# Gate rows stored block by block, and stores moved from SyncE's queue to those of GpSimd and ScalarE, in a hybrid HGRN2, mLSTM and mixture-of-experts layer

## The chip, the core and the metric

The kernel runs on one core of a Trainium2 chip. The core has five engines with a queue of instructions each: TensorE (PE in the profile; the loading of its weights is shown apart, as PEld), VectorE (DVE), ScalarE (ACT), GpSimd (POOL) and SyncE (SP, which here only issues transfers). Transfers between the memory of the chip (DRAM) and the core's own memory run on 16 DMA engines. The metric is the device time of one execution in microseconds: 1577.56 us, the median of three runs (1577.32, 1577.56 and 1581.70).

## The reference

The layer takes 1024 latent tokens `x` and 256 context tokens, each 1024 wide. It projects them with one wide matrix, and runs two kinds of recurrence over the tokens, forward and backward, four heads of HGRN2 and four of mLSTM. The context gives the states from which the latent tokens' recurrences start. Cut to what matters here, the mLSTM is:

```python
def mlstm_scan(q, k, v, log_i, log_f, state):      # chunk by chunk, running-max stabiliser m
    ...
    b = jnp.cumsum(fc, axis=-1)
    d = jnp.where(mask, b[..., :, None] - b[..., None, :] + ic[..., None, :], -jnp.inf)
    inter = b + m[..., None]
    m_row = jnp.maximum(inter, jnp.max(d, axis=-1))
    w_inter = jnp.exp(inter - m_row)
    qk = jnp.einsum('bhid,bhjd->bhij', qc, kc) * jnp.exp(d - m_row[..., None])
    num = jnp.einsum('bhij,bhjv->bhiv', qk, vc) + w_inter[..., None] * jnp.einsum('bhid,bhdv->bhiv', qc, c)
    ...
    h = num / jnp.maximum(jnp.abs(den), jnp.exp(-m_row))[..., None]
```

What follows it:

```python
hg = _head_rms_norm(hg_o_f + hg_o_b) * silu(pr['hg_g'])         # first gates
ml = _head_layer_norm(ml_h_f + ml_h_b) * sigmoid(pr['ml_o'])    # second gates
x = x + g1 * (concat([hg, ml]) @ w_out)
v_x = rms_norm(x, norm2_w) * (1.0 + sc2) + sh2
x = x + g2 * ec_moe(v_x, ...)       # 16 experts, each takes the 128 tokens that score it highest
return rms_norm(x, final_norm_w)
```

Tokens go through the kernel in eight blocks of 128 (`cc` = 0 to 7); a chunk of the reference is half a block, and the kernel uses the same sums over whole blocks.

## The kernel before, in words

The work is staged as follows, in the order of time; TensorE works in all of them.

1. Up to 180 us: the modulation vectors, the context's projections and its final states. `ml_gates` (L389) computes, for all 1024 latent tokens, 8 directions and heads at once, the row `M` = -m_row (eight rows of 1024, kept as 64 partitions of 128) and `em` = exp(M + m), and stores them to DRAM as `d_nm` and `d_em` (L457, L461), [8 rows, 1024 tokens].
2. 180 to 500 us: the HGRN2 heads. Beside them `out_gate(0, ...)` computes the first gates, 128 tokens by 256 columns at a time, into a tile `gsg` of three buffers, and stores each with L719 to `d_go`.
3. 500 to 711 us: the convolutions, the mLSTM's values, the second gates (`out_gate(1, ...)`, L719 again), and the backward states `Sb`, one a block, which `back_u` stores to `d_sb` (L852). The list `ORD` (L1076) interleaves these. Its end takes in `S0`, `O0`, `L0` and `S1`: the first pieces of stage 4.
4. 711 to 935 us: eight rounds, one a block. `scores` (L931) loads `qkx`, `E` and `MB` for a block. `E` takes the block's 128 tokens of the eight rows of `d_nm`, spread to all 128 partitions, and `MB` the same of `d_em` (L936). ScalarE and VectorE make decays of them (L942 to L947). `outputs` (L950) multiplies them with values and states on TensorE (L972, L973) and loads one backward state (L956). `normed` (L981) takes the layer norm, whose power -0.5 GpSimd computes (`rsqrt`, L156, a tile `r4` of 4 columns). `mixed` (L995) loads the HGRN2 outputs and the gates (L998, L999) and puts both halves together. `mixer` (L1012) multiplies with `w_out` (48 matmuls at L1023), adds to `x`, and stores the block to `d_acc` (L1026). `router` (L1043) scales the block with another power on GpSimd (`r2`, 1 column), and stores the experts' input to `d_v` (L1053). In round `cc`, `scores(cc + 2)`, `outputs(cc + 1)` and `mixer(cc)` run.
5. 895 to 968 us: the sorting that picks 128 tokens for each expert. It begins within the last rounds.
6. 968 to 1580 us: the experts. Rows of `d_v` are gathered, and results added into `d_acc`, by transfers that GpSimd issues (L1315, L1311). The experts' weights (L891) are read ahead from stage 4 on into every buffer that has come free. The last rows are normed and written.

Each engine, and each queue of transfers, goes through its instructions in the order in which they stand. A transfer's issue waits in its queue until what it reads is there and its buffer is free, and what stands behind it in that queue waits too. The order within each engine is set when the program is built, by a scheduler that plays the program through with its own costs; so an edit can move instructions on engines that it doesn't name. `load` (L44) is SyncE's queue, for loads and stores alike; SyncE computes nothing. In all 16 transfers fetch `E` and `MB`, of 512 KB each, as 1024 pieces of 512 bytes: `E` and `MB` have two buffers each.

Of the kernel before, what the change touches and what calls it, by code (L numbers as in the profile page):

```python
# [9 lines left out]
F32 = mybir.dt.float32  # L10
# [9 lines left out]
P = 128  # L20
# [12 lines left out]
def tile_hybrid_block(ctx, tc, x, c, cx, c_ctx, ada_w, ada_b, norm1_w, w_in, conv_w, conv_b,  # L33
                      lb_logits, gate_b, hg_norm_w, ml_norm_w, w_out, norm2_w, router_w,
                      e_gate, e_up, e_down, final_w, out, dbg=None, stop=None):
    nc = tc.nc
# [4 lines left out]
    load = nc.sync.dma_start  # L41
# [10 lines left out]
    d_gxc = dram.tile([16, 256], F32, name="d_gxc")  # L52
    d_sb = dram.tile([8, P, 516], F32, name="d_sb")
    d_gx = dram.tile([16, 1024], F32, name="d_gx")
    d_nm = dram.tile([8, 1024], F32, name="d_nm")
    d_em = dram.tile([8, 1024], F32, name="d_em")
    d_g = dram.tile([4, 1024], F32, name="d_g")
    d_v = dram.tile([1024, 1024], F32, name="d_v")
    d_acc = dram.tile([1024, 1024], F32, name="d_acc")
# [330 lines left out]
    def ml_gates(pool):  # L390
# [62 lines left out]
        V.tensor_scalar(M, cm, mcol, None, op0=OP.max)  # L453
        V.tensor_add(b, b, M)
        V.tensor_scalar(M, M, -1.0, None, op0=OP.mult)
        for d in range(2):
            load(d_nm[4 * d:4 * d + 4].rearrange("h (c i) -> (h c) i", i=P), M[64 * d:64 * d + 32])  # L457
        em = mk("gem")
        S.activation(em, M, AF.Exp, bias=mcol)
        for d in range(2):  # L460
            load(d_em[4 * d:4 * d + 4].rearrange("h (c i) -> (h c) i", i=P), em[64 * d:64 * d + 32])  # L461
        pt = bank("ms")
        T.transpose(pt[:, 0:128], g, ident)
        T.transpose(pt[:, 128:256], b, ident)
# [186 lines left out]
    with tc.tile_pool(name="hgp", bufs=1) as hp_:  # L651
        tl = lambda name, shape, bufs: hp_.tile([P] + shape, F32, name=name, tag=name, bufs=bufs)
        fw = {}
        for h in range(4):
            if h % 2 == 0:
                wq = wload([(HG_Q + h * P, 256)])
            w = wload([(HG_FF + h * P, P), (HG_FF + 512 + h * P, P)])
            ada_next(2 if h > 1 else 1)
            F = [tl("hgf", [2, 512], 2) for _ in range(2)]
            QK = [tl("hgqk", [2, 512], 2) for _ in range(2)]  # L660
            for d in range(2):
                pf = [bank("mm"), bank("mm")]
                feat(w, d * P, (d + 1) * P, pf, uh, ul)
                for hf in range(2):
                    hg_f(hp_, F[hf], pf[hf], d, h, slice(0, 512))
            pq = [bank("mm"), bank("mm")]
            feat(wq, (h % 2) * P, (h % 2 + 1) * P, pq, uh, ul)
            for hf in range(2):
                S.activation(QK[hf][:, 1, :], pq[hf], AF.Sigmoid)
                V.tensor_mul(QK[hf][:, 0, :], QK[hf][:, 1, :], pq[hf])  # L670
            Qs, As, Us, decs = [], [], [], []
            for hf in range(2):
                f, qk = F[hf], QK[hf]
                K, Q = tl("hgK", [2, 512], 2), tl("hgQ", [2, 512], 3)
                A, U = tl("hgA", [4, P], 3), tl("hgU", [4, 2, P], 3)
                V.tensor_scalar(K, f, -1.0, 1.0, op0=OP.mult, op1=OP.add)
                V.tensor_add(qk[:, 1, :], K[:, 0, :], K[:, 1, :])
                V.tensor_mul(Q, qk[:, 0, :].unsqueeze(1).to_broadcast([P, 2, 512]), view(f, 512, [[-512, 2], [1, 512]]))
                dec = hg_tree(hp_, f, K, Q, qk, A)
                hg_u(hp_, K, lambda cc: hv[:, 4 * hf + cc, h * P:(h + 1) * P], U, ((0, 4 - hf), (1 - hf, 4)))  # L680
                Qs.append(Q), As.append(A), Us.append(U), decs.append(dec)

            def st(d, cc):

                return S0[:, d, h, :] if cc < 0 or cc > 7 else Us[cc // 4][:, cc % 4, d, :]

            for cc in range(7):
                step(st(0, cc), st(0, cc - 1), decs[cc // 4](0, cc % 4), st(0, cc))
            for cc in reversed(range(1, 8)):
                step(st(1, cc), st(1, cc + 1), decs[cc // 4](1, cc % 4), st(1, cc))  # L690
            for hf in range(2):
                po = bank("ms", [P, 4, P])
                for c4 in range(4):
                    cc = 4 * hf + c4
                    ts = slice(c4 * P, (c4 + 1) * P)
                    T.matmul(po[:, c4, :], As[hf][:, c4, :], hv[:, cc, h * P:(h + 1) * P], start=True, stop=False)
                    T.matmul(po[:, c4, :], Qs[hf][:, 1, ts], st(0, cc - 1), start=False, stop=False)
                    T.matmul(po[:, c4, :], Qs[hf][:, 0, ts], st(1, cc + 1), start=False, stop=True)
                ob = tl("hgo", [4, P], 1)
                for c4 in range(4):  # L700
                    S.activation(ob[:, c4, :], po[:, c4, :], AF.Square, scale=KSCALE,
                                 accum_out=hgr[:, 4 * hf + c4, h:h + 1])
                S.copy(ob, po)
                load(d_hg[4 * hf:4 * hf + 4, :, h * P:(h + 1) * P].rearrange("c p v -> p c v"), ob)

        def out_gate(gi, hf, w, ts):

            for t in ts:
                if gi == 0 and t % 4 == 3:
                    ada_next()  # L710
                pb = bank("mm")
                tok(w, 0, 256, pb[:, :256], t, uh, ul)
                sg = wring.tile([P, 256], F32, name="gsg", tag="gsg", bufs=3)
                if gi:
                    S.activation(sg, pb[:, :256], AF.Tanh, scale=0.5)
                else:
                    S.activation(sg, pb[:, :256], AF.Sigmoid)  # L717
                    V.tensor_mul(sg, sg, pb[:, :256])
                load(d_go[t][:, 512 * gi + 256 * hf:512 * gi + 256 * hf + 256], sg)  # L719

        for hf in range(2):
            out_gate(0, hf, wload([(HG_G + 256 * hf, 256)]), range(8))
# [121 lines left out]
    def back_u(cc):  # L844

        prev = Sbs[-1]
        Sb = tp("Sb", [4, 129], 2)
        for hp, u in enumerate(ml_u(kts.pop(cc), v1[cc])):
            for q in range(2):
                h = 2 * hp + q  # L850
                step(Sb[:, h, :], prev[:, h, :], wsx[:, cc, 1, h:h + 1], u[:, q, :])
        load(d_sb[cc], Sb.rearrange("p h v -> p (h v)"))  # L852
        Sbs.append(Sb)

    Sbs = [mlc[:, 1]]
# [75 lines left out]
    def scores(cc):  # L931

        qk, MB, E = tl("qkx", [8, P], 2), tl("MB", [8, P], 2), tl("E", [2, 4, P], 2)
        load(qk, d_qk[cc])
        for t, src in ((E.rearrange("p d h t -> p (d h) t"), d_nm), (MB, d_em)):
            load(t, bass.AP(tensor=src.tensor, offset=src.offset + cc * P, ap=[[0, P], [1024, 8], [1, P]]))  # L936
        pq = bank("hg", [P, 4, P])
        for h in range(4):
            T.matmul(pq[:, h, :], qk[:, 4 + h, :], qk[:, h, :], start=True, stop=True)
        for d in range(2):  # L940
            for h in range(4):
                S.activation(E[:, d, h, :], E[:, d, h, :], AF.Identity, bias=gT[:, cc, d, h:h + 1])  # L942
            V.tensor_tensor(E[:, d], E[:, d], cmask[:, d, :].unsqueeze(1).to_broadcast([P, 4, P]), op=OP.min)
        S.activation(E, E, AF.Exp)
        for d in range(2):
            V.tensor_mul(MB[:, 4 * d:4 * d + 4, :], qk[:, 0:4, :], MB[:, 4 * d:4 * d + 4, :])
            V.scalar_tensor_tensor(E[:, d], pq, KSCALE, E[:, d], op0=OP.mult, op1=OP.mult)  # L947
        kt = ml_k_tok(blk, lambda h: qk[:, 4 + h, :], wkx[:, cc, 0], False) if cc < 7 else None
        return E, MB, kt
# [63 lines left out]
    def mixer(cc, mh, ml_):  # L1013

        row = slice(cc * P, (cc + 1) * P)
        xm = tb("xm", [1024], 2)
        load(xm, x[row])
        for hf in range(2):
            cs = slice(512 * hf, 512 * hf + 512)
            pb = bank("mm")  # L1020
            for k in range(8):
                for q, (l, r) in enumerate(((mh, woh), (mh, wol), (ml_, woh))):
                    T.matmul(pb, l[:, k, :], r[k][:, cs], start=(k == 0 and q == 0), stop=(k == 7 and q == 2))  # L1023
            V.tensor_mul(pb, pb, g1b[:, cs])
            V.tensor_add(xm[:, cs], xm[:, cs], pb)
        load(d_acc[row], xm)  # L1026
        return xm

    def logits(xm):
# [14 lines left out]
    def router(cc, xm):  # L1044

        row = slice(cc * P, (cc + 1) * P)
        r2 = tb("r2", [1], 2)
        vt = tb("vt", [1024])
        S.activation(vt, xm, AF.Square, scale=1.0 / 32, accum_out=r2)
        rsqrt(r2, r2, 1)  # L1050
        V.scalar_tensor_tensor(vt, xm, r2, A2b, op0=OP.mult, op1=OP.mult)
        V.tensor_add(vt, vt, B2b)
        kept["v"] = load(d_v[row], vt)  # L1053
        if dbg and "xm" in dbg:
            nc.sync.dma_start(dbg["xm"][row], xm)
            nc.sync.dma_start(dbg["v"][row], vt)
        return r2
# [389 lines left out]
```

## Time and profile before

| | |
|---|---|
| median of the runs | 1577.56 us (1577.32 to 1581.70) |
| the profiled execution's own time | 1582.25 us |
| its span, first to last instruction | 1580.4 us |
| TensorE busy, matmuls | 1443.7 us (91%) |
| VectorE, ScalarE, GpSimd busy | 1231.1, 841.8 and 85.6 us |
| chain that ended last | PE 74%, DMA 11%, DVE 8% |
| two lines of that chain | `MB<-d_em` 5%, `E<-d_nm` 2% |

The profile is one execution. A line names the source line, the engine, the operation, the tile written and the tiles read (`out<-in`). Where an engine sat idle, the line names what ended the idle time, as "<-ACT whi L253"; "issue" is time in which nothing that the profile shows was waited for. The chain of waits is followed back from the last instruction. "PEclk" is the clock that TensorE was granted, as a share of its full one. "DMA share" is the mean busy share of the 16 DMA engines; beside GB/s it tells whether busy engines moved much. "SPq" is an instruction of SyncE that issues a transfer; its time is that of the issue, and not of the transfer. A busy TensorE is not TensorE at its peak, since neighbouring matmuls overlap in the records.

### The profile page before, as it was taken

What the parts mean: (1) busy time and instruction counts of PE and PEld (TensorE: products, weight loads), DVE (VectorE), ACT (ScalarE), POOL (GpSimd) and SP (SyncE); (2) the same over time, 40 slices, a digit from 0 to 9 for tenths busy, and PEclk for the clock granted to TensorE, in tenths of its full rate; (3) what the DMA queues carried; (4) which work ended last, traced back from release to release, by engine and by line L of the source; (5) the groups of instructions that cost most, each with busy time, mean ns of one, the idle gap of its engine ahead of it and who ended that gap; (6) DMA issues with size and microseconds to landing.
All of it is one profiled execution on the core that took longest, in us unless ns stands there. A gap on an engine that the chain in (4) does not pass through costs nothing.

```text
span 1580.4 us, 23097 instructions
## 1 busy us (share of the span) xinstructions
PE 1443.7 (91%) x8121; PEld 1202.8 (76%) x8121; DVE 1231.1 (78%) x2223; ACT 841.8 (53%) x1431; POOL 85.6 (5%) x96
## 2 busy tenths in 40 slices
PE   7999999999999999868676965999999999999996
PEld 2899888888898887856565843888888888888774
DVE  3685477888768788447545796999999999998887
ACT  3764434334423323235333323877777878777765
POOL 0000000000020000000000000000100000000003
PEclk9999999999999999979798986999999999999998
DMA  9741311121235343587774386999999999999942
GB/s 258 259 129 31 109 54 54 55 81 55 80 119 162 107 132 115 156 148 221 219 139 152 135 302 215 358 383 384 378 378 386 387 388 386 386 381 357 354 146 107
DMA packets 189616, 341.53 MB, mean 216 GB/s; under 512 B 13720, under 2 KB 116764, under 8 KB 189500
## 3 DMA queue, kind: packets, MB, share of 16 engines
q1 hardware_dynamic: 184888, 324.22, 59.8%
q0 software_dynamic: 4320, 15.73, 4.2%
q8 instruction: 64, 1.05, 0.3%
q14 instruction: 52, 0.43, 0.1%
q10 hardware_dynamic: 292, 0.10, 0.0%
HBM read 307.58 MB, written 32.42 MB: 215 GB/s over the span
## 4 chain that ended last, share of the span: by engine, by line
PE 74%; DMA 11%; DVE 8%; issue 4%; ACT 2%; POOL 1%; SPq 0%; ACTq 0%; POOLq 0%; DVEq 0%
PE mm L1300 21%; PE mm L279 14%; PE mm L287 11%; PE hg L1300 10%; DMA MB<-d_em 5%; PE hg L351 4%; DMA E<-d_nm 2%; PE hg L216 2%; PE ms L1285 2%; DMA sb<-d_sb 1%; PE ms L383 1%; PE mm L1023 1%; PE mm L500 1%; PE hg L1390 1%; PE mm L972 1%
## 5 line engine op out<-in xcount | busy, mean ns | idle before, releaser
L287 PE MATMUL mm<-whi,uh 128*128 128x256 f32 (+1 forms) x512 | 145.4, 284 | 1.5 <-DVE utmp L199 0.9
L287 PE MATMUL mm<-whi,ul 128*128 128x256 f32 (+1 forms) x512 | 145.0, 283 | 0.0
L287 PE MATMUL mm<-wlo,uh 128*128 128x256 f32 (+1 forms) x512 | 144.9, 283 | 0.0
L254 DVE TENSOR_TENSOR wlo<-wraw,whi 128x512 fp32r<-128x512 f32 x96 | 64.9, 689 | 44.9 <-ACT whi L253 43.4
L287 PEld LDWEIGHTS mm<-whi,uh 128*128 128x128 f32 x512 | 96.7, 189 | 3.5 <-DVE utmp L199 1.1
L287 PEld LDWEIGHTS mm<-whi,ul 128*128 128x128 f32 x512 | 96.8, 189 | 0.0
L287 PEld LDWEIGHTS mm<-wlo,uh 128*128 128x128 f32 x512 | 96.3, 188 | 0.3
L826 DVE SCALAR_TENSOR_TENSOR cacc<-pad,cols,cacc 128x1024 f32<-128x1024 f32 x64 | 81.8, 1281 | 14.3 <-ACT cacc L824 13.5
L1300 PE MATMUL mm<-qkx,xT 128*128 128x512 f32 x256 | 83.7, 408 | 0.6 <-ACT xT L1286 0.3
L253 ACT CAST whi<-wraw 128x512 fp32r<-128x512 f32 x96 | 58.3, 620 | 47.1 <-PE mm L279 31.3
L1300 PE MATMUL mm<-E,xT 128*128 128x512 f32 x256 | 81.3, 399 | 0.4 <-ACT E L921 0.4
L1300 PE MATMUL mm<-MB,xT 128*128 128x512 f32 x256 | 80.8, 397 | 0.0
L345 ACT COPY hgc<-hgK 128x512 f32<-128x512 f32 x56 | 35.5, 636 | 68.7 <-PE hg L351 43.5
L351 PE MATMUL hg<-hgQ,hgc 128*128 128x128 f32 x448 | 65.5, 290 | 2.2 <-ACT gsg L717 2.2
L351 PEld LDWEIGHTS hg<-hgQ,hgc 128*128 128x128 f32 x448 | 57.8, 191 | 10.5 <-issue 5.2
L279 PE MATMUL mm<-ul,whi 128*128 128x512 f32 x192 | 63.4, 403 | 0.0
L279 PE MATMUL mm<-uh,whi 128*128 128x512 f32 x192 | 63.1, 405 | 0.0
L279 PE MATMUL mm<-uh,wlo 128*128 128x512 f32 x192 | 62.4, 400 | 0.0
L1300 PEld LDWEIGHTS mm<-E,xT 128*128 128x128 f32 x256 | 47.9, 189 | 13.7 <-ACT E L921 1.7
L360 DVE COPY_PREDICATED hgA<-lm,hg 128x512 f32<-128x512 uint8 x56 | 41.6, 743 | 20.1 <-PE hg L351 16.4
L1300 PEld LDWEIGHTS mm<-MB,xT 128*128 128x128 f32 x256 | 48.2, 188 | 11.9
L298 DVE SCALAR_TENSOR_TENSOR ac<-wraw,csil,ac 128x256 f32<-128x256 f32 x112 | 53.7, 479 | 4.6 <-DMA wraw<-in_ada_w_dram 2.8
(598 smaller groups left out, 4172.4 us busy)
## 6 DMA issues: line engine op xcount, KB each, us to landing
wraw<-in_w_in_dram SPq DMA_DIRECT2D x48, 512.0 KB
wl<-in_exp_w_up_dram SPq DMA_DIRECT2D x34, 512.0 KB
wh<-in_exp_w_up_dram SPq DMA_DIRECT2D x34, 512.0 KB
wh<-in_exp_w_gate_dram SPq DMA_DIRECT2D x34, 512.0 KB
wl<-in_exp_w_gate_dram SPq DMA_DIRECT2D x34, 512.0 KB
wraw<-in_ada_w_dram SPq DMA_DIRECT2D x32, 512.0 KB
wl<-in_exp_w_down_dram SPq DMA_DIRECT2D x29, 512.0 KB
wh<-in_exp_w_down_dram SPq DMA_DIRECT2D x29, 512.0 KB
```

Source lines behind the costliest of these rows:

```text
L216: T.matmul(pm[0:2, :256], csil[:, k, :], adas[i, k // 4][:, k % 4, :, :], start=(k == 0), stop=(k == 7))
L253: S.copy(hi[:, :, cs], src)
L254: V.tensor_sub(lo[:, :, cs], src, hi[:, :, cs])
L279: T.matmul(o, l, r[:, k, i * n:(i + 1) * n], start=(k == 0 and q == 0), stop=(k == 7 and q == 2))
L287: T.matmul(o, l[:, k, ts], r, start=(k == 0 and q == 0), stop=(k == 7 and q == 2))
L298: V.scalar_tensor_tensor(ac, a2[:, k % 4, :], csil[:, k, 0:1], ac, op0=OP.mult, op1=OP.add)
L345: S.copy(view(kc, 0, [[h, 2], [2 * h, 256 // h], [1, h]]), view(K, 0, [[512 + h, 2], [2 * h, 256 // h], [1, h]]))
L351: T.matmul(pb[:, cc, :], kc[:, cc * P:(cc + 1) * P], view(Q, cc * P, pat), start=True, stop=True)
L360: V.copy_predicated(A, lmask[h].unsqueeze(1).to_broadcast([P, 4, P]), scores(h))
L826: V.scalar_tensor_tensor(acc, tap(t), tapw(t, r), acc, op0=OP.mult, op1=OP.add)
L1285: T.transpose(pt[:, k, :], view(src, 4 * q + k, [[8, P]]), ident)
L1300: T.matmul(o, l[:, k, :], r[:, 512 * j:512 * j + 512], start=(k == 0 and p_ == 0), stop=(k == 7 and p_ == 2))
```

## The change

Two things are changed. The rows `d_nm` and `d_em` are kept as [8 blocks, 8 rows, 128 tokens], so that what one block needs is one run of 4 KB, and a load of `E` or `MB` reads that run for each partition; the destination is written as one run too. Writing the rows in this layout takes 16 stores of 8 partitions each, where 4 stores of 32 partitions did it before, and GpSimd issues them. And the stores of the gates, of the backward states, of the blocks after the mixer and of the experts' input are no longer issued by SyncE: GpSimd issues the first gates, `d_sb`, `d_acc` and `d_v`, and ScalarE the second gates. What is computed doesn't change.

```diff
-    d_nm = dram.tile([8, 1024], F32, name="d_nm")
-    d_em = dram.tile([8, 1024], F32, name="d_em")
+    d_nm = dram.tile([8, 8, P], F32, name="d_nm")
+    d_em = dram.tile([8, 8, P], F32, name="d_em")
...
         V.tensor_scalar(M, M, -1.0, None, op0=OP.mult)
-        for d in range(2):
-            load(d_nm[4 * d:4 * d + 4].rearrange("h (c i) -> (h c) i", i=P), M[64 * d:64 * d + 32])
         em = mk("gem")
         S.activation(em, M, AF.Exp, bias=mcol)
-        for d in range(2):
-            load(d_em[4 * d:4 * d + 4].rearrange("h (c i) -> (h c) i", i=P), em[64 * d:64 * d + 32])
+        for t, dst in ((M, d_nm), (em, d_em)):
+            for d in range(2):
+                for h in range(4):
+                    G.dma_start(dst[:, 4 * d + h, :], t[64 * d + 8 * h:64 * d + 8 * h + 8])
...
-                load(d_go[t][:, 512 * gi + 256 * hf:512 * gi + 256 * hf + 256], sg)
+                (nc.scalar if gi else nc.gpsimd).dma_start(d_go[t][:, 512 * gi + 256 * hf:512 * gi + 256 * hf + 256], sg)
...
-        load(d_sb[cc], Sb.rearrange("p h v -> p (h v)"))
+        G.dma_start(d_sb[cc], Sb.rearrange("p h v -> p (h v)"))
...
-        for t, src in ((E.rearrange("p d h t -> p (d h) t"), d_nm), (MB, d_em)):
-            load(t, bass.AP(tensor=src.tensor, offset=src.offset + cc * P, ap=[[0, P], [1024, 8], [1, P]]))
+        for t, src in ((E.rearrange("p d h t -> p (d h t)"), d_nm), (MB.rearrange("p a t -> p (a t)"), d_em)):
+            load(t, bass.AP(tensor=src.tensor, offset=src.offset + cc * 1024, ap=[[0, P], [1, 1024]]))
...
-        load(d_acc[row], xm)
+        G.dma_start(d_acc[row], xm)
...
-        kept["v"] = load(d_v[row], vt)
+        kept["v"] = G.dma_start(d_v[row], vt)
```

On SyncE's queue, at the end of stage 3, the first two blocks' loads stood between stores of gates (L719) and states (L852). Before:

```order
L852 DMA d_sb<-Sb 128x516
L934 DMA qkx<-d_qk 128x1024
L852 DMA d_sb<-Sb 128x516
L936 DMA E<-d_nm 128x8x128
L719 DMA d_go<-gsg 128x256
L936 DMA MB<-d_em 128x8x128
L934 DMA qkx<-d_qk 128x1024
L719 DMA d_go<-gsg 128x256
L936 DMA E<-d_nm 128x8x128
L719 DMA d_go<-gsg 128x256
L936 DMA MB<-d_em 128x8x128
```

On the same queue at the same place, after the change:

```order
L1072 DMA wor<-in_w_out_dram 128x1024 x3
L306 DMA gsg<-in_ada_b_dram 1x256
L934 DMA qkx<-d_qk 128x1024
L936 DMA E<-d_nm 128x1024
L936 DMA MB<-d_em 128x1024
L934 DMA qkx<-d_qk 128x1024
L936 DMA E<-d_nm 128x1024
L936 DMA MB<-d_em 128x1024
```

The loads now stand together, and no store is ahead of them or among them.

On GpSimd in the rounds of stage 4, only the powers of `normed` (`r4`, 4 columns) and `router` (`r2`, 1 column) stood. Before:

```order
L156 TENSOR_TENSOR r4_6691<-r4_6691,mhalf_136 128x4
L156 TENSOR_TENSOR r4_7090<-r4_7090,mhalf_136 128x4
L156 TENSOR_TENSOR r2_7298<-r2_7298,mhalf_136 128x1
L156 TENSOR_TENSOR r4_7330<-r4_7330,mhalf_136 128x4
L156 TENSOR_TENSOR r2_7533<-r2_7533,mhalf_136 128x1
L156 TENSOR_TENSOR r4_7565<-r4_7565,mhalf_136 128x4
```

The same powers on GpSimd after the change (buffer numbers differ), with the stores of the mixer's blocks (L1026) and of the experts' input (L1053):

```order
L156 TENSOR_TENSOR r_6703<-r_6703,mhalf 128x4
L156 TENSOR_TENSOR r_7102<-r_7102,mhalf 128x4
L1026 DMA d_acc<-xm 128x1024
L156 TENSOR_TENSOR r_7310<-r_7310,mhalf 128x1
L1053 DMA d_v<-vt 128x1024
L156 TENSOR_TENSOR r_7342<-r_7342,mhalf 128x4
L1026 DMA d_acc<-xm 128x1024
L156 TENSOR_TENSOR r_7545<-r_7545,mhalf 128x1
L1053 DMA d_v<-vt 128x1024
L156 TENSOR_TENSOR r_7577<-r_7577,mhalf 128x4
```

Each store of `d_v` now stands right ahead of the power that the next block's layer norm waits for, and each store of `d_acc` ahead of the power of the same block's `router`.

## Rows read from the trace of the kernel before

**Rows 1.** Lines of the page: the span, the granted clock and the share of the DMA engines in 40 equal slices of 39.5 us, and the packets of the DMA queues.

```profile
span 1580.4 us, 23097 instructions
...
PEclk9999999999999999979798986999999999999998
DMA  9741311121235343587774386999999999999942
...
DMA packets 189616, 341.53 MB, mean 216 GB/s; under 512 B 13720, under 2 KB 116764, under 8 KB 189500
```

**Rows 2.** Stretches in us from the span's start: their length, busy time of TensorE, its weight loads, VectorE, ScalarE and GpSimd (with the number of instructions), granted clock, DMA share, GB/s.

```profile
743.87:883.12 139.25, 100.22 (x549) 85.07 (x550) 72.55 (x214) 50.72 (x145) 6.51 (x8) 0.84 0.64 162
666.00:711.00 45.00, 25.88 (x189) 24.29 (x190) 16.62 (x48) 18.40 (x53) 1.42 (x1) 0.81 0.76 143
0.00:100.00 100.00, 89.88 (x574) 63.03 (x575) 56.21 (x137) 59.73 (x120) 5.25 (x17) 0.97 0.80 242
...
968.00:1520.00 552.00, 549.59 (x2566) 443.19 (x2567) 520.43 (x568) 430.73 (x511) 37.90 (x30) 0.99 0.97 360
```

**Rows 3.** The chain that ended last, pieces of it between 640 and 900 us: start, length, what.

```profile
666.36 15.29 DMA E<-d_nm
...
739.34 18.56 DMA MB<-d_em
...
761.55 18.62 DMA sb<-d_sb
...
788.22 19.94 DMA MB<-d_em
...
818.25 15.66 DMA MB<-d_em
...
847.01 17.52 DMA MB<-d_em
...
883.19 11.15 PE mm L1023 x48
```

**Rows 4.** Who waited for whom between 590 and 900 us: us in total, times, longest.

```profile
ACT E L942 <- DMA E<-d_nm: 44.6, 7, 8.4
DVE MB L946 <- DMA MB<-d_em: 36.7, 7, 7.0
```

**Rows 5.** TensorE in order of time: start, length, instruction, count, and in brackets the idle time before it.

```profile
673.73 1.12 PE L484 MATMUL ms<-ident,qkx 128*128 128x128 f32 x4 [5.66 <-DMA qkx<-d_qk]
684.69 1.66 PE L500 MATMUL mm<-v,mkt 128*128 128x129 f32 x6 [9.84 <-ACT mkt L488]
...
743.87 0.50 PE L1023 MATMUL mm<-wh,mh 128*128 128x512 f32 x1 [0.89 <-DVE hsum L978]
...
876.55 0.39 PE L972 MATMUL mm<-v,E 128*128 128x129 f32 x2
876.77 0.39 PE L973 MATMUL mm<-sb,MB 128*128 128x129 f32 x2
...
883.12 0.50 PE L1023 MATMUL mm<-wh,mh 128*128 128x512 f32 x1
```

**Rows 6.** SyncE's queue in order of time: start and length of the issue, line, transfer.

```profile
725.18 0.42 SPq L875 DMA_DIRECT2D B2b<-d_g  x1
...
738.53 0.72 SPq L936 DMA_DIRECT2D E<-d_nm  x1
739.34 1.77 SPq L936 DMA_DIRECT2D MB<-d_em  x1
```

**Rows 7.** Stretches of 4 us, columns as in rows 2.

```profile
726.00:730.00 4.00, 3.23 (x15) 2.36 (x14) 2.66 (x9) 2.73 (x4) 0.20 (x1) 1.00 0.96 348
730.00:734.00 4.00, 3.69 (x15) 2.45 (x14) 2.37 (x3) 2.69 (x5) 0.81 (x1) 1.00 0.99 381
...
746.00:750.00 4.00, 4.00 (x19) 3.30 (x19) 0.08 (x1) 0.18 (x1) 0.00 (x0) 1.00 0.98 51
750.00:754.00 4.00, 4.00 (x20) 3.30 (x19) 0.69 (x1) 2.52 (x9) 0.00 (x0) 1.00 1.01 66
```

**Rows 8.** GpSimd in order of time: start, length, line, operation, and in brackets the idle time before it.

```profile
463.30 5.41 POOL L724 TENSOR_TENSOR hgr<-hgr,mhalf 128x32 f32<-128x32 f32 x1 [352.54 <-DVE hgr L723]
...
763.67 1.02 POOL L156 TENSOR_TENSOR r<-r,mhalf 128x4 f32<-128x4 f32 x1 [21.44 <-DVE r L155]
...
790.87 1.01 POOL L156 TENSOR_TENSOR r<-r,mhalf 128x4 f32<-128x4 f32 x1 [20.24 <-DVE r L155]
...
1500.17 1.57 POOL L1311 DMA_INDIRECT d_acc<-go,idx  x1 [36.38 <-DVE go L1308]
1501.70 0.64 POOL L1348 IOTA wh<- 128x512 f32 x1
```

**Rows 9.** The instructions that touch the tensor `d_acc`, last line of that view: time from issue to landing of the transfers that GpSimd issued.

```profile
DMA to landing us min/median/max: 6.4/7.9/9.6
```

**Rows 10.** VectorE in order of time, the second of the two instructions that make block 0's `vt`, which L1053 stores.

```profile
744.32 1.22 DVE L1052 TENSOR_TENSOR vt<-vt,B2b 128x1024 f32<-128x1024 f32 x1
```

**Rows 11.** What SyncE's queue waited for between 590 and 900 us: us in total, times, longest.

```profile
SPq L719 <- ACT gsg L715: 37.5, 13, 8.5
```

**Rows 12.** The instructions that touch the tile `gsg`: an issue by SyncE and one by ScalarE, count, duration in ns (least, median, most), first and last start.

```profile
L719 SPq DMA_DIRECT2D d_go<-gsg x32: 319/324/1113, 413.7 to 710.8; - x32
...
L312 ACTq DMA_DIRECT2D d_g<-gsg x16: 221/222/231, 260.5 to 688.0; - x16
```

## The prediction

> **What bounds the kernel now.** I read the page first, then stretches, then the chain of waits, then each queue in order of time. In the page's slices the granted clock is full but for slices 16 to 24, and there the DMA engines are mostly well used as well [rows 1]: the place to look at is about 640 to 970 us. The experts' stage, 552 us long, has TensorE busy 549.6 and the DMA engines at 97% [rows 2]; nothing in it is edited, its buffers are full before it begins, and I let it move as one piece. In the four rounds from the start of mixer 1 (743.87) to that of mixer 5 (883.12) TensorE is busy 100.2 of 139.25 us at a mean clock of 0.84, VectorE 72.6, ScalarE 50.7: no engine is full [rows 2]. What ends the idle time is in the chain: one transfer after another of `E`, `MB` and `sb`, 15 to 20 us each [rows 3]. ScalarE waits 44.6 us for `E`, VectorE 36.7 us for `MB`, seven times each [rows 4]. Both then stand in order with everything behind them, and TensorE waits for them in turn: between 666 and 711 us it idles 19.1 us (45 less 25.9) [rows 2], 5.66 of it for a `qkx` that lies in the queue behind the first `E` and `MB`, and 9.84 for a ScalarE that is itself held by the second `E` [rows 3 to 5].
>
> **The loads.** `E` and `MB` of a block are issued at 738.5 and 739.3 [rows 6]. From 746 to 754 the DMA engines are busy 98 to 101% and move 51 to 66 GB/s [rows 7]: 1.05 MB at 60 GB/s is 17.5 us, which is the chain's 15 to 20. The form after the change (4 KB runs, each read by all partitions) is in the trace once as well: `B2b`, 512 KB of one row of 4 KB, issued at 725.18 [rows 6]. The engines then move 348 and 381 GB/s at 96 and 99% [rows 7], with `B2b` and its twin `A2b` among the loads; two loads at 60 GB/s would have shown there. At 350 GB/s a pair takes 3.0 us of the DMA engines, 14.5 less than now, eight times.
>
> Here a rule of the Trainium skill speaks against the change. "DMA: Bandwidth & Descriptors", section Specifications, gives 512 bytes as the least transfer for full rate; by it the old pieces were already large enough, the slowness has another cause, and the sum would be that of the second rival below. The start of the kernel agrees with the rule in part: its modulation weights come in 512-byte pieces too, and 242 GB/s at a share of 0.80 [rows 2] is no 60. So size alone is not the reason; that eight runs 4 KB apart are read again and again by every partition must be part of it, and the new layout takes that away as well.
>
> **The end of stage 3.** The two waits of 5.66 and 9.84 go, since `E` and `MB` no longer fill the queue and no store of a gate stands ahead of them. Of the 19.1 us idle I take away 14, for the two waits make 15.5. Least 5, if the scores' chain of ScalarE and VectorE holds TensorE instead; most 19.
>
> **The four rounds.** They hold 549 matmuls: 4 x 48 at L1023, which follow one another so that 48 take 11.15 us [rows 3], and 357 others. Two L972 start 0.22 us before the next two [rows 5], so 0.11 each: 39.3 us. At full clock a round's matmuls are 11.15 + 9.8 = 20.9 us. This is the least. Now a round takes 139.25 / 4 = 34.8 [rows 5]. From above I take the best round there is, 27.2 us from one power of `normed` to the next (763.67 to 790.87) [rows 8]. Between 20.9 and 27.2 I choose 23.5: loads in time leave the chain of a block (power, ScalarE's norm, VectorE's mix, transposes), which runs beside the other block's 11 us of matmuls, and a few gaps remain. 4 x 23.5 = 94.0, so 45 us go (55.7 at 20.9, 30.4 at 27.2). Next late in a round will be the buffer of `E`, free only when the block two before has been used.
>
> **What is added.** GpSimd issues 16 stores of rows, 16 of gates, 7 of states, 8 of `d_acc` and 8 of `d_v`. The rows of before show no plain store on this engine; the nearest are its scatters of 128 rows of 4 KB, 1.57 us [rows 8], landing 6.4 us after the issue at the soonest [rows 9]. GpSimd is held for the first and not for the second: it begins another instruction 1.53 us after the start of a scatter (1500.17, 1501.70) [rows 8].
> - In a round, `d_v`'s store stands ahead of the next `r4`. What it waits for ended at 745.54 (744.32 + 1.22) [rows 10], and the `r4` came at 763.67 [rows 8]: room for 1.6 us, also if the round gets 11 us shorter. `d_acc` waits for the sum that `r2` waits for too, through ScalarE's squares, which take longer than the issue. I count 2 us; at most 7 x 1.6 = 11, if the room is gone.
> - The first gates' tenth store stands behind the power at L724, 5.41 us from 463.30 [rows 8]. Three buffers cover it but for about 1 us; at most 5.4.
> - The row stores, 16 x 1.57 = 25 us on an idle engine, are needed 480 us later: nothing. The states have two buffers each, nothing.
> - ScalarE issues 16 gate stores at 0.2 to 0.33 us [rows 12], 5.3 us at most, in a stretch where it is busy 18 of 45 [rows 2]: 1 us.
> In all 4 us, at most 22; below nothing only by what the queue gains. SyncE's 37.5 us of waits for gates [rows 11] are not TensorE's time: what they cost is the lateness of the loads behind them, counted above.
>
> Here the rule of "DMA: Bandwidth & Descriptors", section Issuing engines are not separate DMA queues, agrees with counting no transfer time: spreading DMAs over engines saves only the issue. No row here shows more.
>
> **The sum.** -14 - 45 + 4 = -55 against the profiled execution's 1582.25: 1527.2. That execution lies 4.7 above the median of 1577.56, so 1522.5 for the median. With all bounds on one side: -19 - 55.7 = -74.7, that is 1503; and -5 - 30.4 + 22 = -13.4, that is 1564.
>
> **Rivals.**
> 1. *The rounds keep another limit.* The loads become quick, but the chain within a block takes over, and rounds stay at the best that is seen, 27.2; of stage 3's idle only 8 goes. -8 - 30.4 + 4 = -34: 1543. For it: no engine is full in the rounds, and VectorE and ScalarE wait for each other. Against: the long waits are nearly all transfers [rows 3, 4].
> 2. *The change doesn't do it: the load stays slow*, since all partitions still read the same bytes. What is left is the loads' earlier issue, two blocks by some 3 us each: -7, 1570. For it: the start's 512-byte pieces are fast. Against: `B2b` [rows 6, 7].
> 3. *Slower: GpSimd holds the powers back.* If a store keeps the engine until it has landed, and not for 1.6 us, two stores stand before each block's norm, 15.8 us a round by the median landing of 7.9 [rows 9]. Rounds of 23.5 + 15.8 = 39.3 are 4.5 longer than now (+18); three further powers are late by 15.8 as well, of which some 8 each shows (+24); stage 3 gives its 14: 1605. It decides from a hold of about 4 us a store (59 us over 16 stores). Against: GpSimd is free after 1.6 us, with VectorE busy 520 of 552 [rows 2, 8].
>
> For the third rival the Trainium skill has a mechanism, the trap that "SBUF — State Buffer" describes in its section "SBUF: two separate sides": GpSimd writes the descriptors itself, and can't while VectorE runs an operation in a mode that takes the shared port. The scatter's row doesn't show it. By the page it would be plain copies and scalar operations that do this, and the rounds are mostly operations on two tensors.
>
> **How the numbers follow.** The forecast 0.70, rival 1 0.17, rival 2 0.06, rival 3 0.07. The likeliest time is 1522. The forecast's own range is 1503 to 1540; it is widened to 1500, for a gain in the round before 743.87 that I count as none, and to 1553, so that rival 1 is in with 10 us to spare. A measurement of this kernel tells 0.3%, about 5 us, from no change. Faster by more than that: the forecast, rival 1, and half of rival 2, 0.90. Same: 0.03. Slower: 0.07.
>
> **What would show it.** The DMA packets fall by about 14,300 (16 loads, 1024 pieces to 128), from 189,616 [rows 1]. The waits for `E` and `MB` fall from 44.6 and 36.7 us to under 10 each. Mixer 1 to mixer 5 takes 84 to 109 us, and the clock in it is over 0.95. Between the gates' end and the rounds TensorE idles about 5 us. On GpSimd a store takes 1 to 2 us, and no `r4` comes more than 2 us after the VectorE instruction before it. The experts' stage is as long as before. The prediction is wrong if the loads still move under 100 GB/s with full engines, if a round stays over 27 us, or if the gain of the rounds is paid back in the sorting or in the experts' stage.

## The result, and the profile after

The changed kernel takes 1507.92 us (median of four runs, 1506.98 to 1509.19). Beside it on the same chip the kernel before took 1577.48, so the ratio is 0.9553 [0.9536, 0.9571]: faster by 4.5%, about 70 us. The forecast was 1522 us, 55 us less than before; the time lies inside the range of 1500 to 1553, and inside the likeliest case's own range. The profiled execution took 1506.98 us, with a span of 1505.2, which is 75.2 less than the span of before.

The lines of the changed kernel's page that answer to [rows 1]:

```profile
span 1505.2 us, 23166 instructions
...
PEclk9999999999999999999999969999999999999998
DMA  9841411230316336277954669999999999999932
...
DMA packets 173616, 341.53 MB, mean 227 GB/s; under 512 B 14040, under 2 KB 98652, under 8 KB 173500
```

The granted clock no longer sags in slices 16 to 24; one slice in the sorting is left at 6. The same bytes move (341.53 MB), in 16,000 packets fewer.

Stretches of the changed kernel, with the columns of [rows 2]: the four rounds from mixer 1 to mixer 5, the 4-us stretches behind the issue of a pair of loads, and from the first gather of expert rows to the end:

```profile
717.89:804.73 86.84, 86.08 (x534) 72.79 (x535) 69.05 (x209) 49.72 (x142) 11.83 (x16) 1.00 0.67 235
...
716.00:720.00 4.00, 3.13 (x18) 2.60 (x17) 3.72 (x7) 4.00 (x15) 0.40 (x2) 1.00 1.02 384
720.00:724.00 4.00, 4.00 (x19) 3.30 (x19) 3.78 (x9) 1.80 (x3) 0.43 (x1) 1.00 1.02 409
886.43:1505.20 618.77, 591.29 (x2744) 474.34 (x2744) 568.76 (x629) 464.75 (x571) 56.90 (x48) 0.98 0.91 337
```

Four rounds took 139.25 us [rows 2] and take 86.84, with TensorE busy for 86.08 of them and the clock at 1.00: the rounds are now TensorE's own work. The engines that moved 51 to 66 GB/s for `E` and `MB` [rows 7] now move 384 and 409.

The chain that ended last, changed kernel, pieces of it between 710 and 816 us (start, length, what):

```profile
710.15 7.35 DMA kin<-d_hg
...
717.89 5.75 PE mm L1023 x24
...
741.23 11.12 PE mm L1023 x48
761.52 11.17 PE mm L1023 x48
784.51 11.14 PE mm L1023 x48
804.80 11.12 PE mm L1023 x48
```

Where one transfer of 15 to 20 us followed another [rows 3], the mixers' matmuls stand. Who waited for `E` and `MB` between 560 and 840 us (us in total, times, longest), against 44.6 and 36.7 [rows 4]:

```profile
DVE MB L946 <- DMA MB<-d_em: 10.6, 3, 4.3
ACT E L942 <- DMA E<-d_nm: 7.5, 6, 3.7
```

The end of stage 3, from 664.5 us on. TensorE and the clock in the kernel before, in the 21.5 us that open with the wait for `E`, and in what follows:

```profile
664.50:686.00 21.50, 5.08 (x32) 4.25 (x31) 5.52 (x11) 9.65 (x28) 0.00 (x0) 0.66 0.63 118
686.00:719.16 33.16, 25.90 (x197) 24.05 (x196) 18.59 (x55) 13.98 (x37) 1.42 (x1) 0.96 0.77 163
```

TensorE idles 16.4 of the 21.5 us, and the granted clock goes to half (1.2 of 2.4 GHz; 0.50 in each stretch of 2 us from 672 to 686) once it has stood for these loads. The second line is the rest of the way to the mixer of round 0. In the changed kernel TensorE's idle times from here to the mixer of round 0, all of them (in brackets, with what ended them):

```profile
665.35 0.49 PE L939 MATMUL hg<-qkx 128*128 128x128 f32 x2 [0.73 <-DVE gsg L307]
...
671.14 1.16 PE L973 MATMUL mm<-sb,MB 128*128 128x129 f32 x8 [1.29 <-DMA sb<-d_sb]
...
673.55 0.39 PE L287 MATMUL mm<-whi,uh 128*128 128x256 f32 x1 [0.58 <-DVE hsum L978]
...
691.89 1.07 PE L1008 MATMUL ms<-ident,mix 128*128 128x128 f32 x4 [2.24 <-issue]
...
693.23 0.65 PE L1008 MATMUL ms<-ident,mix 128*128 128x128 f32 x4 [0.28 <-DVE mix L1003]
```

They make 5.1 us, and the clock stays full. The same way in the changed kernel, which has done as many matmuls at 661.0 as the kernel before at 664.5:

```profile
661.00:693.64 32.64, 27.51 (x226) 25.99 (x225) 21.34 (x62) 17.91 (x50) 1.99 (x2) 1.00 0.48 159
```

GpSimd in order of time in one round of the changed kernel, against [rows 8]:

```profile
712.22 0.59 POOL L1026 DMA_DIRECT2D d_acc<-xm  x1 [7.37 <-DMA wor<-in_exp_w_gate_dram]
715.68 0.57 POOL L156 TENSOR_TENSOR r<-r,mhalf 128x1 f32<-128x1 f32 x1 [2.86 <-DVE r L155]
719.85 0.58 POOL L1053 DMA_DIRECT2D d_v<-vt  x1 [3.60 <-DVE vt L1052]
726.85 1.04 POOL L156 TENSOR_TENSOR r<-r,mhalf 128x4 f32<-128x4 f32 x1 [6.42 <-DVE r L155]
```

A store holds the engine 0.58 us, and the engine idles before each power, until VectorE has what the power reads: no power waits for a store, in this round or the others.

The span's 75.2 us, from these landmarks: the start of mixer 0 comes 25.5 us earlier (719.16, now 693.64); of this some 3.5 had been gained by 664.5 us (where from wasn't traced) and 22 come at the end of stage 3. Mixer 0 to 1 gives 0.5, the four rounds 52.4. From mixer 5 to the first gather it takes 1.3 longer (80.43, now 81.70), and from there to the end 1.9 longer (616.85, now 618.77).

### The profile page after: what moved, and what is told of

Its sections match the earlier page's. It is cut to its first block, busy times and chain, and to the rows that moved or that the text cites. A ratio compares the mean times of both kernels' runs of the same rounds, so it can differ in the third digit from the quotient of the medians.

```text
span 1505.2 us, 23166 instructions
## 1 busy us (share of the span) xinstructions
PE 1423.3 (95%) x8121; PEld 1187.7 (79%) x8121; DVE 1231.0 (82%) x2223; ACT 841.7 (56%) x1431; POOL 118.0 (8%) x151
## 2 busy tenths in 40 slices
DMA packets 173616, 341.53 MB, mean 227 GB/s; under 512 B 14040, under 2 KB 98652, under 8 KB 173500
## 4 chain that ended last, share of the span: by engine, by line
PE 68%; issue 16%; DVE 8%; DMA 4%; ACT 2%; POOL 1%; SPq 0%; ACTq 0%; POOLq 0%; DVEq 0%
PE mm L1300 22%; PE hg L1300 11%; PE mm L279 10%; PE mm L287 6%; PE mm L1023 4%; PE hg L351 4%; PE hg L216 2%; PE ms L1285 2%; PE ms L383 1%; DVE ac L298 1%; DMA wraw<-in_ada_w_dram 1%; PE hg L1390 1%; DVE qkx L922 1%; PE hg L1039 1%; DMA Sb<-in_exp_w_up_dram 0%
## 5 line engine op out<-in xcount | busy, mean ns | idle before, releaser
L360 DVE COPY_PREDICATED hgA<-lm,hg 128x512 f32<-128x512 uint8 x56 | 41.6, 743 | 18.4 <-PE hg L351 16.4
```

What stands on the lines that cost most here:

```text
L360: V.copy_predicated(A, lmask[h].unsqueeze(1).to_broadcast([P, 4, P]), scores(h))
```

## The experiments

Two questions were open: which part of the change brings the gain, and what made the old loads slow. My theory was the distance of 4 KB between eight pieces that every partition reads again; the rivals were the size of the pieces, their number, and the queue on which the stores stand. Times are medians, each beside runs of the kernel before on the same chip, whose median was 1572 to 1575 us there. Beside the changed kernel it was 1577.48, so times from two such sets of runs are comparable to some 5 us and no closer.

**The layout alone.** All stores back on SyncE's queue, block layout kept:

```diff
-                    G.dma_start(dst[:, 4 * d + h, :], t[64 * d + 8 * h:64 * d + 8 * h + 8])
+                    load(dst[:, 4 * d + h, :], t[64 * d + 8 * h:64 * d + 8 * h + 8])
...
-        G.dma_start(d_acc[row], xm)
+        load(d_acc[row], xm)
```

> The block layout alone, all stores on SyncE's queue. Theory (the gain is the loads of E and MB getting quick): 1508 to 1518 us, and the loads' waits under 15 us in all. Rival (the gain is a SyncE queue without stores): over 1550 us.

Measured: 1508.63 us, ratio 0.9589 [0.9572, 0.9605]. `E` is waited for 6.3 us in all between 560 and 840 us, and for `MB` no wait stands in the view. The four rounds:

```profile
718.56:809.21 90.65, 87.91 (x550) 74.48 (x550) 71.97 (x214) 51.19 (x145) 6.91 (x8) 1.00 0.70 243
```

They hold 16 matmuls more than after the whole change (550 against 534). The whole gain, as closely as these runs tell, is there without moving a store.

**The stores alone.** Old layout, stores moved as in the change:

```diff
-        load(d_acc[row], xm)
+        G.dma_start(d_acc[row], xm)
...
-        load(d_sb[cc], Sb.rearrange("p h v -> p (h v)"))
+        G.dma_start(d_sb[cc], Sb.rearrange("p h v -> p (h v)"))
```

> The stores moved, the rows kept as before. Theory: 1568 to 1580 us, with the DMA engines full at 50 to 70 GB/s while E and MB come in. Rival (a SyncE queue without stores): under 1530 us.

Measured: 1577.45 us, ratio 1.0023 [1.0009, 1.0036]. Its waits between 590 and 900 us, and one stretch of 4 us in which the loads are moved:

```profile
DVE MB L946 <- DMA MB<-d_em: 58.4, 7, 14.7
...
ACT E L942 <- DMA E<-d_nm: 43.5, 8, 8.6
```

```profile
762.00:766.00 4.00, 1.09 (x4) 0.72 (x4) 1.30 (x2) 0.68 (x2) 0.00 (x0) 0.50 0.97 67
```

The loads are as slow as before, 67 GB/s at a share of 0.97, and they are waited for no less: `MB` for 58.4 us against 36.7, `E` for 43.5 against 44.6 [rows 4]. The move is worth nothing here.

**Small pieces in a block.** The whole change, but the pieces are 512 bytes again, 1024 in a load, and lie 1 KB apart:

```diff
-    d_nm = dram.tile([8, 8, P], F32, name="d_nm")
+    d_nm = dram.tile([8, 8, 2 * P], F32, name="d_nm")
...
-            load(t, bass.AP(tensor=src.tensor, offset=src.offset + cc * 1024, ap=[[0, P], [1, 1024]]))
+            load(t, bass.AP(tensor=src.tensor, offset=src.offset + cc * 2048, ap=[[0, P], [256, 8], [1, P]]))
```

> As the changed kernel, but a block's eight rows lie 1 KB apart, so that each load still is 1024 pieces of 512 bytes. If the 4 KB pitch between the pieces made the loads slow: 1506 to 1518 us. If the number or the size of the pieces did: 1560 to 1580 us, and 50 to 70 GB/s at full engines.

**Padded rows.** The old layout, with 128 unused floats behind each row, so 4608 bytes between the pieces in place of 4096; stores moved. Against the changed kernel:

```diff
-    d_nm = dram.tile([8, 8, P], F32, name="d_nm")
+    d_nm = dram.tile([8, 1152], F32, name="d_nm")
...
+            load(t, bass.AP(tensor=src.tensor, offset=src.offset + cc * P, ap=[[0, P], [1152, 8], [1, P]]))
```

> Eight rows of all 1024 tokens as before, but with a pitch of 4608 bytes and not 4096; stores moved, pieces of 512 bytes. If the pitch of 4 KB made the loads slow: 1506 to 1520 us. If the number or the size of the pieces, or their spread over more than one 4 KB run, did: 1560 to 1580 us.

Measured: with pieces 1 KB apart 1506.44 us, ratio 0.958 [0.956, 0.9601]; with padded rows 1506.51, 0.9575 [0.9559, 0.9591]. Both make 187952 packets, nearly what the kernel before made. Behind the issue of a pair of loads, first the kernel with pieces 1 KB apart, then the one with padded rows:

```profile
716.00:720.00 4.00, 3.13 (x18) 2.53 (x17) 4.00 (x8) 4.00 (x14) 0.45 (x1) 1.00 1.02 402
720.00:724.00 4.00, 4.00 (x19) 3.34 (x18) 3.78 (x9) 1.50 (x3) 0.13 (x1) 1.00 1.05 409
```

```profile
716.00:720.00 4.00, 3.41 (x15) 2.84 (x16) 4.00 (x10) 3.58 (x11) 0.58 (x1) 1.00 1.03 415
720.00:724.00 4.00, 4.00 (x20) 3.30 (x19) 3.78 (x11) 0.93 (x2) 0.00 (x0) 1.00 1.07 369
```

The engines move as much as with one run of 4 KB. Neither the size nor the number of the pieces was the cause; the distance was.

**Other distances.** Padded rows with 8192 bytes from row to row, and pieces in a block 2048 bytes apart; nothing else differs from the two kernels just shown:

```diff
-    d_nm = dram.tile([8, 1152], F32, name="d_nm")
+    d_nm = dram.tile([8, 2048], F32, name="d_nm")
...
-            load(t, bass.AP(tensor=src.tensor, offset=src.offset + cc * P, ap=[[0, P], [1152, 8], [1, P]]))
+            load(t, bass.AP(tensor=src.tensor, offset=src.offset + cc * P, ap=[[0, P], [2048, 8], [1, P]]))
```

> The kernel with padded rows again (512-byte pieces, stores moved), only the distance between the eight pieces of a row is 8192 bytes instead of 4608. Theory A (what slows the loads is a distance that is a large power of two: pieces that far apart are served by the same part of the memory, and 128 partitions ask for the same eight): the loads are at least as slow as before, 1565 to 1600 us, waits for MB and E in the mixing stage of 40 us or more each, and stretches of 4 us with the DMA engines over 0.9 busy at under 100 GB/s. Theory B (only 4096 bytes is bad, for instance because pieces then stand in one page after the other at the same place of a page): 1503 to 1512 us, as with 4608 bytes. Theory C (the further the pieces lie apart, the slower, whatever the number): the 4608-byte kernel would already have been slow, so C would be left only if 8192 came out between the two, near 1540.

```diff
-    d_nm = dram.tile([8, 8, 2 * P], F32, name="d_nm")
+    d_nm = dram.tile([8, 8, 4 * P], F32, name="d_nm")
...
-            load(t, bass.AP(tensor=src.tensor, offset=src.offset + cc * 2048, ap=[[0, P], [256, 8], [1, P]]))
+            load(t, bass.AP(tensor=src.tensor, offset=src.offset + cc * 4096, ap=[[0, P], [512, 8], [1, P]]))
```

> The kernel with 512-byte pieces in a block again (stores moved), only the distance between the eight pieces is 2048 bytes instead of 1024. Theory A (the eight pieces share a part of the memory when they lie a power of two apart, and the smaller the distance the more parts they spread over): between the two, 1508 to 1545 us; I take 1520, with the loads of 4 us stretches at 100 to 250 GB/s while the engines are over 0.9 busy. Theory B (4096 bytes is a step: below it nothing is lost): 1503 to 1512 us, and stretches at about 400 GB/s as with 1024 bytes.

Measured: 8192 bytes give 1626.24 us, ratio 1.0323 [1.0302, 1.0344]: slower than the kernel before, and above what theory A allowed. The chain of that kernel, three pieces between 770 and 870 us:

```profile
774.07 24.44 DMA E<-d_nm
...
811.88 21.49 DMA MB<-d_em
...
847.76 20.47 DMA MB<-d_em
```

The pieces are longer than those of 4096 bytes [rows 3], and four rounds take 163.5 us. Its waits between 560 and 960 us, and a stretch of 4 us behind the first of these loads:

```profile
ACT E L944 <- DMA E<-d_nm: 94.2, 8, 15.8
DVE MB L948 <- DMA MB<-d_em: 76.6, 7, 21.7
```

```profile
788.00:792.00 4.00, 1.08 (x4) 0.71 (x4) 1.30 (x2) 0.18 (x1) 0.00 (x0) 0.50 0.26 69
```

The waits are as theory A has them, but the engines are not over 0.9 busy, as it expected: they are at 0.26 while 69 GB/s move. 2048 bytes give 1511.84 us, ratio 0.9606 [0.9584, 0.9627], which is in the ranges of both theories. Its stretches behind a pair of loads are quick, and not at the 100 to 250 GB/s that A expected; yet its waits for `MB` and `E` are more than with 1 KB (11.4 and 8.0 us), and four rounds take 90.7 us against 86.8:

```profile
717.00:721.00 4.00, 3.14 (x17) 2.56 (x17) 3.94 (x8) 4.00 (x15) 0.41 (x2) 1.00 0.96 356
721.00:725.00 4.00, 4.00 (x20) 3.30 (x19) 3.77 (x8) 1.57 (x3) 0.20 (x1) 1.00 1.05 401
```

```profile
DVE MB L946 <- DMA MB<-d_em: 19.1, 5, 7.2
ACT E L942 <- DMA E<-d_nm: 15.5, 5, 5.0
```

So there is a small loss at 2048 bytes by the trace; the intervals of the two ratios overlap, and whether it is a slope or a step below 4096 stays open. Theory B, that only 4096 is bad, falls with 8192; C, that it is worse the further apart, falls with 4608. That it must be a power of two, and not just a multiple of 4096, was not tried: 12288 bytes, for one, would tell.

**The distance alone, on the kernel before.** Every store stays on SyncE's queue:

```diff
-    d_nm = dram.tile([8, 1024], F32, name="d_nm")
+    d_nm = dram.tile([8, 1152], F32, name="d_nm")
...
+                load(d_nm[4 * d + h, 0:1024].rearrange("(c i) -> c i", i=P), M[64 * d + 8 * h:64 * d + 8 * h + 8])
...
-            load(t, bass.AP(tensor=src.tensor, offset=src.offset + cc * P, ap=[[0, P], [1024, 8], [1, P]]))
+            load(t, bass.AP(tensor=src.tensor, offset=src.offset + cc * P, ap=[[0, P], [1152, 8], [1, P]]))
```

> The kernel before with nothing else than 128 unused floats behind each of the eight rows of the two gate tables (4608 bytes from row to row instead of 4096), and sixteen row stores in place of four, all stores on SyncE's queue as before. If the distance alone is the cause and where the stores are issued is worth nothing: 1503 to 1513 us, ratio 0.955 to 0.962, mixer 1 to mixer 5 in 84 to 92 us. If the block layout or the moved stores are needed as well: 1530 us or more.

Measured: 1508.05 us, ratio 0.9583 [0.9562, 0.9603], mixer 1 to mixer 5 in 91.0 us. 512 bytes of padding a row, with the row stores split from 4 into 16, bring all that the change brings. The split is not what does it: the kernel with 8192 bytes has the same sixteen stores and is slow.

**Is repetition needed?** `E` and `MB` are read from expert weights, 512-byte pieces 4096 bytes apart. In the first kernel each partition reads its own eight rows, in the second all read the same eight. Both leave out the gates' decay and its bias in the mixing, so only their time can be read. The second against the first:

```diff
         for t, src in ((E.rearrange("p d h t -> p (d h) t"), e_gate[0]), (MB, e_up[0])):
-            load(t, bass.AP(tensor=src.tensor, offset=src.offset + cc * P, ap=[[8192, P], [1024, 8], [1, P]]))
+            load(t, bass.AP(tensor=src.tensor, offset=src.offset + cc * P, ap=[[0, P], [1024, 8], [1, P]]))
```

> The changed kernel, but E and MB are loaded from two tables of expert weights, every partition from eight rows of its own: eight 512-byte pieces 4096 bytes apart, 1024 pieces in a load as before, none read twice in one load. (Left out: the gates' decay and its bias in the mixing; the values loaded in their place mean nothing.) Theory A (the 4096 bytes slow a load only because 128 partitions ask for the same eight pieces, which sit in a small part of the memory): 1503 to 1515 us, and 4 us stretches after the loads' issue at 300 GB/s or more. Rival (a distance of 4096 bytes between a load's pieces is slow by itself, repeated or not): as before, 1560 to 1590 us, with stretches under 100 GB/s at busy engines.

> As the kernel of the first run of this call (same two tables, same 512-byte pieces 4096 bytes apart, same part left out), but every partition reads the same eight rows, as the gate rows are read. Both theories: as before, 1560 to 1590 us, with stretches under 100 GB/s at busy engines. If it came out near 1508 us, the slow loads would belong to the small scratch tables and not to distance and repetition, and the other run could not be read.

Measured: own rows 1506.65 us, ratio 0.9579 [0.9561, 0.9598]; the same rows 1576.5, 1.0017 [1.0005, 1.0029]. Stretches in which the loads are moved, first of own rows, then of the same rows:

```profile
716.00:720.00 4.00, 3.13 (x16) 2.52 (x16) 4.00 (x8) 3.94 (x14) 0.58 (x1) 1.00 1.02 404
720.00:724.00 4.00, 4.00 (x20) 3.30 (x19) 3.78 (x9) 1.43 (x2) 0.00 (x0) 1.00 1.07 392
```

```profile
759.00:763.00 4.00, 1.15 (x4) 0.56 (x4) 1.56 (x5) 1.65 (x4) 1.04 (x1) 0.57 0.35 77
763.00:767.00 4.00, 0.88 (x4) 0.48 (x3) 0.26 (x1) 0.00 (x0) 0.00 (x0) 0.50 0.31 72
```

One number in an access pattern, the step from partition to partition, is the difference. The distance slows the loads only where the same pieces are read over and over. In the first kernel, too, all pieces lie whole multiples of 4096 bytes apart, but they are 1024 different ones spread over 4 MB, and in the second eight in 32 KB; whether it is the reading again or the small stretch of memory that matters isn't separated. And since the weights behave as the scratch tables do, it isn't a matter of those tables, nor of data just written. In the second kernel the engines are not even busy (0.31 to 0.35) while little moves.

**What is left in the rounds.** Mixer 0 to mixer 1 takes 24.3 us, the next four rounds 21.7 on the average, and three loads of expert rows stand ahead of that round's score loads; the chain shown above has a transfer of `kin` (the HGRN2 outputs that `mixed` loads) behind them, 7.35 us. Put later, against the changed kernel:

```diff
-            raw_load(3)
...
-            raw_load(1)
+            raw_load(4 if cc == 1 else 1)
```

> The changed kernel, with the three loads of expert rows that SyncE issues in round 0 ahead of the second round's score loads put into round 1, behind its score loads. In the changed kernel the round from mixer 0 to mixer 1 takes 24.3 us and the next ones 21.7. Theory A (the three loads, 6.2 us at SyncE's head in front of E, MB and kin, are what makes that round longer): 2 to 3 us come off, 1505 us, and mixer 0 to 1 falls to about 22 us. Theory B (in that round the extra work of the router's set-up on TensorE and VectorE is the length): within 1 us of the changed kernel, 1508 us, or up to 2 us slower where the loads now collide with later ones.

Measured: 1508.22 us, ratio 0.9576 [0.9558, 0.9593], the changed kernel's time. Mixers 0, 1 and 2 start at 694.74, 722.30 and 741.93: the first round is 27.6 us and the second 19.6, 47.2 together against 47.5. The time is the one that theory B gives, though B's reason isn't shown: the edit also spread TensorE's work in another way (141 and 120 matmuls in these two rounds, 126 and 144 in the changed kernel). None of these kernels beats the changed one by more than can be measured.

## Why the prediction was right

The gain was larger than forecast by 15 us, and each step can be set beside its measurement.

- *The loads.* Right, with their cause. The step "eight runs 4 KB apart are read again and again by every partition must be part of it" is shown from both sides: another distance with the same pieces, or the same distance without repetition, gives the whole gain. The Trainium skill's rule in "DMA: Bandwidth & Descriptors", section Specifications (512 bytes are enough for full rate), agrees with these runs: 369 to 415 GB/s in the stretches shown of 512-byte pieces 1024 or 4608 bytes apart. It spoke against the change only if the change is taken for one of sizes. The same page, section "Latency and other measured facts", tells of row distances that are large powers of two, from 512 KiB up, which in copies from DRAM to DRAM cost up to half the rate, and of a padding of 4 KiB that gives it back where 192 bytes don't; it names a sharing of memory channels as an inference. Here the distance is 4 or 8 KB, the loss is to about a sixth (51 to 77 GB/s against some 400), 512 bytes of padding are enough, and a partition's repetition is a condition. That the pieces share a part of the memory is the likely reading of these runs too, but none of them shows it.
- *The end of stage 3*, -14 with bounds of -5 and -19: mis-sized, and outside its bounds. It gave 22 us, and some 3.5 more had come before it. Of the 22, 18.6 are idle time, from 664.5 us (661.0 in the changed kernel) to the mixer of round 0: 23.7 us before, 5.1 now. I had read it in 45 us only, found 19.1 there, and taken away 14. The other 3.5 I had not counted at all: TensorE is busy 31.0 us there before and 27.5 now, for the same work, since the clock had fallen (0.66 over 21.5 us) after TensorE had stood.
- *The four rounds*, -45 with bounds of -30.4 and -55.7: the right mechanism, 7 us too small. A round takes 21.7 us, close to the 20.9 that I worked out as the least. I took 2.6 us a round for gaps; there are 0.2 (86.08 busy of 86.84), and a matmul that isn't the mixer's takes 0.121 us on the average (86.08 less 44.6, over 342) and not 0.11. Of the 52.4 us that went, 38.3 were idle time (39.0, now 0.8), and 14.1 were busy time of TensorE (100.22, now 86.08), which had run at a clock of 0.84 and had 15 matmuls more to do; my 20.9, worked out at full clock, held the clock's part.
- *What is added*, +4: nothing of it is to be seen. The nearest row, a scatter's 1.57 us, was nearly three times too dear for a plain store (0.53 to 0.59 us), and the room before each `r4` was there. The kernels with all stores on SyncE's queue and those with the stores moved lie within about 2 us of each other (1508.63 and 1508.05; 1506.44 and 1506.51).
- *The experts' stage moves as one piece*: nearly. From mixer 5 to the end 3.2 us are paid back (1.3 and 1.9). The first goes with work that the new order puts behind mixer 5: the rounds have 15 matmuls fewer than before, and the stretch behind them 15 more (295, before 280), with TensorE busy 2.1 us longer. What makes the experts 1.9 us longer wasn't tried.

The sum as forecast was -14 - 45 + 4 = -55; as measured, -25.5 - 0.5 - 52.4 + 3.2 = -75.2 in the profiled spans. Since the profiled execution of before lay 4.7 us above its median and that of the changed kernel 0.9 below, 70 us of it are in the medians. The 75.2 are half a microsecond more than all bounds on one side gave (74.7); that the median still lies in the likeliest case's own range is in part luck, by those 4.7 and 0.9 us.

Rival 1 (the rounds keep 27.2 us) falls: with the loads in time TensorE is full, and no chain of ScalarE and VectorE shows. Rival 2 (slow because all partitions read the same bytes) falls as it was put, since runs of 4 KB that all partitions read are quick; but repetition is a condition of the slowness. Rival 3 falls with the stores' 0.58 us; the mechanism that the Trainium skill has for it ("SBUF — State Buffer", "SBUF: two separate sides") doesn't show, with VectorE busy 69 of 87 us beside these stores.

Of the signs, the clock (1.00), the rounds (86.84 in 84 to 109) and the idle time before them (5.1 us for 5) came as written. A store on GpSimd was to take 1 to 2 us and takes 0.58; the experts' stage was to be as long as before and is 1.9 us longer. `E`'s waits are under 10 us and `MB`'s just over (10.6). The packets fell by 16,000 and not by 14,300: the layout alone takes 14,272 away (175344 packets in that kernel), and the rest goes with the moved stores, which I had counted as alike.

## What to carry to other kernels

When loads are waited for and the DMA engines, busy or not, move little, look at the addresses that one load asks for: with a few pieces read by all partitions, the distance between them decides, and 4 KB and 8 KB were the distances to pad away or to lay out side by side. When a wait in front of TensorE goes, count the matmuls behind it at full clock too, and test a bundle of edits one by one: here the stores that were moved were worth nothing, and the distance between the pieces alone was worth 4%.

## What the runs showed of the hardware

Loads of 512 KB, 128 partitions each reading 4 KB, differ in the kernel's time only by where the pieces lie (16 such loads in the kernel; the row of 4608 bytes is the one with moved stores, the last row reads other tables; the times are from four sets of runs, comparable to some 5 us):

| pieces | distance | read by | median, us | ratio to before |
|---|---|---|---|---|
| 4096 bytes | none | all partitions | 1507.92 | 0.9553 |
| 512 bytes | 1024 | all | 1506.44 | 0.958 |
| 512 bytes | 2048 | all | 1511.84 | 0.9606 |
| 512 bytes | 4096 | all | 1577.45 | 1.0023 |
| 512 bytes | 4608 | all | 1506.51 | 0.9575 |
| 512 bytes | 8192 | all | 1626.24 | 1.0323 |
| 512 bytes | 4096 | each its own | 1506.65 | 0.9579 |

In slow loads the DMA engines show as busy to very different shares (0.97 in one stretch, 0.31 in another) at about the same 70 GB/s, so a low share there is no sign of room. And a plain store that GpSimd issues holds it for 0.53 to 0.59 us, also when it has 128 rows of 4 KB, against 1.57 for a scatter of as much.
